# The values of two attention groups as one projection by seven products of quarters

## The chip, the cores and the metric

The kernel runs on one core of a Trainium2 chip. The metric is the device time of one execution in microseconds, as the median of several runs. Beside it stands one profiled execution, whose trace gives every instruction on the engines TensorE (PE; its weight loads are PEld), VectorE (DVE), ScalarE (ACT), GpSimd (POOL) and on the queue of SyncE (SP), which issues the transfers.

## The reference, cut to what matters

One layer of a hybrid decoder over 512 positions of width 1024, in float32. An RMSNorm gives u; one projection `u @ w_in` gives queries, keys and values of 18 attention heads, a pooling input, the inputs of a state-space mixer, and gates. The heads form three groups of six; each group attends with its own dilation:

```
ATTN_GROUPS = ((128, 1), (512, 4), (2048, 16))     # window, dilation
proj = u @ w_in[i]
q, k, v, pool_in, z, xbc, dt_raw, gate_pre = jnp.split(proj, split_idx, axis=-1)
v = v.reshape(b, s, ATTN_HEADS, HEAD_DIM)          # 18 heads of 64: 3 groups of 384 columns
```

The three branches are gated, merged and projected; a gated feed-forward layer and a final norm follow. What matters here is v: for each group, 512 x 1024 of u times 1024 x 384 of the weights. The text counts groups 1 to 3; the code counts g = 0 to 2.

## The kernel before, in words

**Products in three terms.** TensorE multiplies in a rounded float32 form, so each operand is split into a high part (the rounded value) and a low part (what rounding left), and a product is high x high, high x low and low x high: three matmuls for each block of 128 contracted rows (`mm3`, L222 to L229). u is kept turned, as `uh` and `ul`, eight blocks of 128 features by 512 positions. Weights come from memory per job: `fetch` (L170) issues the transfer into one of two `raw` buffers, `cast` (L182) makes the high part `wh` on ScalarE (L191), `lows` (L204) the low part `wl` on VectorE (L211). There are three buffers for `wh` and two for `wl`.

**Jobs and their pipeline.** The program is a list of jobs in a fixed order, and the order of instructions on TensorE, ScalarE, VectorE and GpSimd is that in which the program writes them. At the head of job n (L1459 to L1482) the loop first issues any half of a cast that is still held back (`second`), then the low part of job n+1, then sets up the cast of job n+2, then issues the transfer of job n+3, and only then writes the body of job n. The cast is cut into two column halves: `flush` (L139), called at the start of each `step`, issues one half; what is left is issued at the head of the next job.

**Steps.** `step()` (L145) lets pieces of other work in between the matmuls: after the flush it advances every generator in `running` by one stage and starts one from `waiting`. The items of attention and of the state-space mixer come in this way. An attention item (`item` in `attend`, L507) has four stages at four steps: scores on TensorE (L521, for a pair of heads at once), bias addition and row maxima on VectorE (L528 to L539), exponentials on ScalarE (L542); nothing; the transpose of the probabilities on TensorE (L548) and its copy by VectorE or ScalarE in turns (L549); for every second head the product with the values (L560). A group of attention ends with transposes of its statistics (L573).

**The order around the change** (`program`, L1277): second gates, the pooling branch and its output projection `w_b`, then per group g its values (`v_jobs`, L454), its queries and keys (`qk_jobs`, L482), and `attend(g)`, which queues the items. After group 1 the state-space preparation is put in as the sixth item that waits; after group 2 come six jobs for the convolved inputs (L673) and `ssd_start` (L842), which issues twelve Silus on ScalarE and queues the state-space items; then group 3's values, queries and keys.

`v_jobs` has two jobs per group, each with four contracted blocks and 384 columns; u is the stationary operand and the weights stream. Each job makes two steps, one after two blocks of positions. In the second job each block's result is copied out of PSUM (L466); those of groups 2 and 3 are scattered by 4 transfers each into `vr` tiles, in the order of the dilation (L477). `qk_jobs` has three jobs per group; each makes one query and one key chunk of 24 matmuls with 512 columns, and a step after each chunk.

**Products by quarters, already in use.** `down` (L1075) computes part of the feed-forward output in the way that the change extends to the values: four quarters of the activations times four quarters of the weights by seven products of sums for eight. `sums_of` (L1055) makes the sums of activations, and `diff` (L1091) those of weights, in place.

Of the kernel before, what the change touches and what calls it, by code (L numbers as in the profile page):

```python
# [10 lines left out]
F32 = mybir.dt.float32  # L11
# [5 lines left out]
P = 128  # L17
# [55 lines left out]
class Job:  # L73


    def __init__(self, parts, k, c, body):
        self.parts, self.k, self.c, self.body = parts, k, c, body
        self.raw = self.split = None
        self.late = self.short = False
        self.load = self.form = None  # L80


@with_exitstack
def trunk(ctx: ExitStack, tc, out, x, rel_bias, ln1_g, w_in, b_gate, w_a, pool_w, pool_scale, w_b,
# [23 lines left out]
    def T(name, dt=F32, shape=(P, S)):  # L108
        return big.tile(list(shape), dt, name=name, tag="t")
# [105 lines left out]
    def low(job, cuts=1, eng=None):  # L215
        for _ in lows(job, cuts, eng):
            pass

    def wsrc(w, k0, k1, c0, c1):
        return w[k0 * P:k1 * P, c0:c1].rearrange("(k p) c -> p k c", p=P)  # L220
# [10 lines left out]
    def chunk_a(ps, ws, j, xh, xl, ks, lo=0, hi=S, k0=0):  # L231
        wh, wl = ws
        mm3(ps[:, lo:hi], lambda k: wh[:, k0 + k, j * P:(j + 1) * P],
            lambda k: wl[:, k0 + k, j * P:(j + 1) * P],
            lambda k: xh(k)[:, lo:hi], lambda k: xl(k)[:, lo:hi], ks)
# [14 lines left out]
    def jobs_b(parts_of, c, xh, xl, nk, evac, kstep=4, mk=None, blocks=range(4), tail=0,  # L250
               turn_over=False, acc=None, opened=(), keep=()):

        acc = {} if acc is None else acc
        starts = list(range(0, nk, kstep))
        held = []

        def use(k0, k1, ws, tb):
            wh, wl = ws  # L260
            mm3(acc[tb][:, :c], lambda k: wh[:, k - k0, :], lambda k: wl[:, k - k0, :],
                lambda k: xh(k, tb), lambda k: xl(k, tb), range(k0, k1),
                k0 == 0 and tb not in opened, k1 == nk and tb not in keep, flip=True)

        for n, k0 in enumerate(starts):
            k1 = min(nk, k0 + kstep)

            def body(ws, n=n, k0=k0, k1=k1):
                if n == 0:
                    for tb in blocks:  # L270
                        if tb not in opened:
                            acc[tb] = (mk or MM)("pb")
                late = n >= len(starts) - tail
                if late:
                    held.append((k0, k1, ws))
                if late and n < len(starts) - 1:
                    return
                for tb in blocks:
                    for a in (held if late else [(k0, k1, ws)]):
                        use(*a, tb)  # L280
                    if k1 == nk and tb not in keep:
                        evac(tb, acc[tb])
                    if tb % 2:
                        step()
            job = Job(parts_of(k0, k1), k1 - k0, c, body)
            job.short = len(blocks) < 4
            if turn_over and n == len(starts) - 1:
                job.late = True

                def body(ws, job=job, inner=body):  # L290
                    late_split.append(job.prepare(later=True))
                    inner(ws)
                job.body = body
            yield job


    def rstd_of(ss, cols, n):
# [156 lines left out]
    def v_jobs(g):  # L454
        extra = SH if g == 0 else 0

        def parts(k0, k1):
            c = C_V + 384 * g
            r = [wsrc(w_in, k0, k1, c, c + 384)]
            if extra:  # L460
                r.append(wsrc(w_in, k0, k1, C_DT, C_DT + SH))
            return r

        def evac(tb, ps):
            t = T(f"v{g}")
            (act.copy if tb % 2 else dve.tensor_copy)(t[:, :384], ps[:, :384])  # L466
            if extra:
                dve.tensor_copy(dtr[:, tb, :], ps[:, 384:400])
            if g == 0:
                V[g, tb] = t  # L470
                return

            if tb == 0:
                for n in range(4):
                    V[g, n] = T(f"vr{g}")
            for n in range(4):
                sp.dma_start(V[g, n][32 * tb:32 * tb + 32, :384], t[n:P:4, :384])  # L477

        return jobs_b(parts, 384 + extra, lambda k, tb: uh[:, k, tb * P:(tb + 1) * P],
                      lambda k, tb: ul[:, k, tb * P:(tb + 1) * P], KD, evac)  # L480

    def qk_jobs(g):  # L482
        for i in range(3):
            def body(ws, i=i):
                for j, which in enumerate("qk"):
                    ps = MM("pqk")
                    chunk_a(ps, ws, j, uhk, ulk, range(KD))
                    t = T(f"{which}{g}")
                    if which == "q":
                        act.mul(grouped(t, g), blocked(ps, g), 0.125)  # L490
                    else:
                        dve.tensor_copy(plain(t, g), perm(ps, g))
                    QK[which, g, i] = t
                    step()
            cq, ck = C_Q + 384 * g + i * P, C_K + 384 * g + i * P
            yield Job([wsrc(w_in, 0, KD, cq, cq + P), wsrc(w_in, 0, KD, ck, ck + P)], KD, 256, body)
# [522 lines left out]
    def up_evac(m, ps):  # L1019
        t = HC[m] = T("hc")  # L1020
        act.activation(t, ps, AF.Identity, bias=ff["c1"][:, ff["b"] + m:ff["b"] + m + 1], scale=fw(2, m))  # L1021
        for k in range(2):
            sh = 2 - k
            dve.scalar_tensor_tensor(t[:, sh:], ps[:, :S - sh], fw(k, m), t[:, sh:], OP.mult, OP.add)  # L1024
        if m < KF:
            act.activation(t, t, AF.Silu)
            return
        a = HC[m - KF]
        pool.tensor_tensor(a, a, t, OP.mult)  # L1029

        def later():
            yield
            k = m - KF
            if k >= KS or k % 2:
                h, l = T("fh", F32R), T("fl", F32R)
                act.copy(h, a)
                dve.tensor_sub(l, a, h.bitcast(F32))
                ACTS[k] = (h, l)
                if k < KS:
                    yield  # L1040
                    for _ in sums_of(k // 2, HC[k - 1], a):
                        yield
                return
            if k == 0:
                wide.extend(ypool.tile([P, 4, S], F32R, name=n, tag="xs") for n in ("sh", "sl"))
            t = T("f0", F32R)
            act.copy(t[:, :256], a[:, :256])
            dve.tensor_sub(t[:, 256:], a[:, :256], t[:, :256].bitcast(F32))
            FS[0, k // 2] = (t[:, :256], t[:, 256:])

        running.append(later())

    FS = {}

    def sums_of(p, f0, f1):  # L1055


        lo, hi = slice(0, 256), slice(256, S)
        sa, sb = T("sa"), T("sb")
        dve.tensor_tensor(sa[:, lo], f0[:, hi], f1[:, hi], OP.add)  # L1060
        dve.tensor_tensor(sa[:, hi], sa[:, lo], f0[:, lo], OP.subtract)
        dve.tensor_tensor(sb[:, lo], f0[:, lo], f0[:, hi], OP.subtract)
        dve.tensor_tensor(sb[:, hi], f1[:, lo], sa[:, hi], OP.subtract)
        yield
        ah, al = (t[:, p, :] for t in wide)
        bh, bl = T("sbh", F32R), T("sbl", F32R)
        act.copy(ah, sa)
        act.copy(bh, sb)
        yield
        dve.tensor_sub(al, sa, ah.bitcast(F32))  # L1070
        dve.tensor_sub(bl, sb, bh.bitcast(F32))
        FS[1, p], FS[2, p] = (ah[:, lo], al[:, lo]), (ah[:, hi], al[:, hi])
        FS[3, p], FS[4, p] = (bh[:, lo], bl[:, lo]), (bh[:, hi], bl[:, hi])

    def down():  # L1075

# [7 lines left out]
        def load_w():  # L1084
# [2 lines left out]
                W[at] = both[:, 4 * at:4 * at + 4, :]  # L1087
                sp.dma_start(W[at], quarter(at, 1))
            get_x1()

        def diff(out, a, b):  # L1091
            dve.tensor_tensor(out, a, b, OP.subtract)
            return out

        def product(ps, ws, parts, first, last):

# [180 lines left out]
    def program():  # L1277
        yield from jobs_a(w_in, C_POOL, 8, uhk, ulk, KD, pool_evac)
        yield Call(lambda: waiting.append(rows_of_bias()))
        yield from gate_jobs(1)  # L1280
        yield from pool_out_job()
        yield from branch_jobs(1, w_b, YB, 8)
        for g in range(3):
            yield from v_jobs(g)
            yield from qk_jobs(g)
            yield Call(lambda g=g: attend(g))
            if g == 0:
                yield Call(lambda: waiting.insert(5, ssd_prep()))
            if g == 1:
                yield from jobs_a(w_in, C_XBC, 12, uhk, ulk, KD, xbc_evac)  # L1290
                yield Call(ssd_start)
# [193 lines left out]
ORDERED = {EngineType.PE, EngineType.Activation, EngineType.DVE, EngineType.Pool}  # L1485
NBIG = 54
MIX = "ZZ0zz1ggggaa"
SSD_ORDER = ((0, 0, 1), (1, 0, 1), (0, 1, 1), (2, 0, 1), (1, 1, 1), (3, 0, 1), (2, 1, 1), (3, 1, 1))
WARM = 12
# [29 lines left out]
```

## Time and profile before

| | us |
|---|---|
| median of 3 runs | 1052.53 (1052.18 to 1053.45) |
| the profiled execution | 1051.72 |
| its span, first to last instruction | 1049.5 |
| PE / DVE / ACT / POOL busy | 1038.3 / 613.5 / 442.4 / 137.8 |
| values of group 1, two jobs | 160.2 to 177.8 |
| queries and keys of group 1 | 177.8 to 210.5 |
| values of group 2, with attention items between | 210.5 to 230.4 |
| values of group 3, with items between | 354.2 to 375.4 |
| queries and keys of group 3 | 375.4 to 415.2 |

Times are in microseconds, those of single rows from the start of the span. A row of the view in order of time gives start, length, engine, line, operation, output and inputs with shapes, the number of instructions that follow each other, and in brackets how long the engine was idle before and what ended that wait. Matmuls are pipelined: the length of one is longer than the distance to the next, so the chain's pieces, not the lengths, give what a matmul costs. Operations that follow each other on VectorE also overlap a little.

### The profile page before, as it was taken

The numbers are of one execution on the slowest core, as the hardware profiler recorded it, in microseconds if no ns is written. First come the engines' busy times: TensorE is split into PE (matmuls) and PEld (weight loads), VectorE is DVE, ScalarE is ACT, GpSimd is POOL, SyncE is SP. The second block draws the span as 40 slices with busy tenths as digits, with TensorE's granted clock in tenths as the row PEclk, the third lists the DMA queues.
The fourth block names the chain that finished last, engine by engine and source line by source line (L and its number), as shares of the span: only waits on it lengthen the run. The fifth ranks groups of instructions, "written<-read, shape, count | busy, mean of one in ns | idle before, by whom it ended". The sixth has DMA issues, their size and how long they took to land.

```text
span 1049.5 us, 13068 instructions
## 1 busy us (share of the span) xinstructions
PE 1038.3 (99%) x5244; PEld 867.5 (83%) x5244; DVE 613.5 (58%) x824; ACT 442.4 (42%) x716; POOL 137.8 (13%) x118
## 2 busy tenths in 40 slices
PE   8999999999999999999999999999999999999997
PEld 8878889897888888787888888898888888878885
DVE  5552523254667548576568856766766556556545
ACT  6343411233444733466554324545444443433331
POOL 1580000000000001100134500001111111110110
PEclk9999999999999999999999999999999999999999
DMA  7236233342222355541253426643232322362332
GB/s 234 86 116 181 81 103 86 95 114 78 84 81 61 81 150 141 151 120 52 81 144 89 156 85 221 206 162 118 80 121 81 110 91 84 117 240 65 115 102 80
DMA packets 119787, 121.80 MB, mean 116 GB/s; under 512 B 5523, under 2 KB 101590, under 8 KB 119727
## 3 DMA queue, kind: packets, MB, share of 16 engines
q1 hardware_dynamic: 119727, 120.98, 37.4%
q8 instruction: 41, 0.67, 0.3%
q14 instruction: 19, 0.16, 0.0%
HBM read 115.07 MB, written 4.32 MB: 114 GB/s over the span
## 4 chain that ended last, share of the span: by engine, by line
PE 94%; issue 2%; ACT 1%; DVE 1%; DMA 1%; POOL 0%; SPq 0%; DVEq 0%; ACTq 0%; POOLq 0%
PE pa L228 35%; PE pu L228 22%; PE pb L228 17%; PE pqk L228 9%; PE p L228 2%; PE ps L521 1%; PE pu L1211 1%; PE ppw L228 1%; PE po L560 1%; PE pt L548 1%; PE py L817 1%; PE pyo L823 1%; DMA raw<-in_w_in_dram 1%; PE pst L834 0%; ACT wh L191 0%
## 5 line engine op out<-in xcount | busy, mean ns | idle before, releaser
L211 DVE TENSOR_TENSOR wl<-raw,wh 128x2048 fp32r<-128x2048 f32 (+3 forms) x95 | 217.3, 2290 | 93.1 <-ACT wh L191 54.2
L191 ACT CAST wh<-raw 128x1024 fp32r<-128x1024 f32 (+3 forms) x188 | 189.4, 1025 | 86.9 <-PE pa L228 32.9
L228 PE MATMUL pa<-uh,wh 128*128 128x512 f32 x384 | 99.3, 400 | 0.3 <-ACT wh L191 0.3
L1024 DVE SCALAR_TENSOR_TENSOR hc<-pu,fcol,hc 128x510 f32<-128x510 f32 x88 | 65.8, 748 | 51.3 <-ACT hc L1021 49.7
L228 PE MATMUL pa<-ul,wh 128*128 128x512 f32 x384 | 95.0, 389 | 0.0
L228 PE MATMUL pa<-uh,wl 128*128 128x512 f32 x384 | 94.9, 389 | 0.0
L228 PEld LDWEIGHTS pa<-ul,wh 128*128 128x128 f32 x384 | 72.1, 188 | 15.3
L228 PEld LDWEIGHTS pa<-uh,wl 128*128 128x128 f32 x384 | 72.1, 188 | 15.0
L228 PEld LDWEIGHTS pa<-uh,wh 128*128 128x128 f32 x384 | 69.9, 188 | 16.5 <-issue 1.7
L228 PE MATMUL pu<-uh,wh 128*128 128x512 f32 (+1 forms) x352 | 83.6, 379 | 0.0
L228 PE MATMUL pu<-uh,wl 128*128 128x512 f32 (+1 forms) x352 | 83.5, 379 | 0.0
L228 PE MATMUL pu<-ul,wh 128*128 128x512 f32 (+1 forms) x352 | 83.5, 379 | 0.0
L228 PEld LDWEIGHTS pu<-uh,wl 128*128 128x128 f32 x352 | 64.2, 188 | 12.5
L228 PEld LDWEIGHTS pu<-ul,wh 128*128 128x128 f32 x352 | 64.2, 188 | 12.5
L228 PEld LDWEIGHTS pu<-uh,wh 128*128 128x128 f32 x352 | 64.1, 188 | 12.4
L1021 ACT ACTIVATE hc<-pu,fcol,fcol 128x512 f32<-128x512 f32 x40 | 31.2, 780 | 75.7 <-PE pu L228 75.5
L1029 POOL TENSOR_TENSOR hc<-hc 128x512 f32<-128x512 f32 x22 | 31.5, 1432 | 223.1 <-DVE hc L1024 169.3
L796 POOL TENSOR_TENSOR xd<-xc,dec 128x512 f32<-128x512 f32 x6 | 6.4, 1064 | 361.6 <-DVE xc L787 343.0
L542 ACT ACTIVATE sb<-sb,nm 128x128 f32<-128x128 f32 (+1 forms) x72 | 30.1, 419 | 47.0 <-DVE nm L539 33.3
L919 DVE TENSOR_TENSOR sg<-sg,pa 128x512 f32<-128x512 f32 x24 | 16.1, 685 | 41.9 <-PE pa L228 41.8
L228 PE MATMUL pqk<-uh,wh 128*128 128x512 f32 x144 | 36.7, 397 | 0.0
L228 PE MATMUL pqk<-ul,wh 128*128 128x512 f32 x144 | 35.6, 389 | 0.0
(322 smaller groups left out, 1695.5 us busy)
## 6 DMA issues: line engine op xcount, KB each, us to landing
raw<-in_w_in_dram SPq DMA_DIRECT2D x25, 1024.0 KB, 5.4
raw<-in_ffn_w_up_dram SPq DMA_DIRECT2D x22, 1024.0 KB, 5.1
raw<-in_w_in_dram SPq DMA_DIRECT2D x20, 512.0 KB, 5.6
raw<-in_ffn_w_down_dram SPq DMA_DIRECT2D x10, 1024.0 KB, 5.1
raw<-in_w_o_dram SPq DMA_DIRECT2D x8, 1024.0 KB, 5.7
raw<-in_w_in_dram SPq DMA_DIRECT2D x6, 768.0 KB
raw<-in_w_b_dram SPq DMA_DIRECT2D x4, 1024.0 KB, 5.0
al<-ad SPq DMA_DIRECT2D x16, 256.0 KB, 6.3
```

Source lines behind the costliest of these rows:

```text
L191: act.copy(job.high[:, :, o], job.raw[:, :, o])
L211: (eng or dve).tensor_tensor(l[:, :, o], job.raw[:, :, o], h[:, :, o].bitcast(F32), OP.subtract)
L228: pe.matmul(ps, l, r, start=first and n == 0, stop=last and n == total - 1)
L521: pe.matmul(pss[i][:, o:o + w * P], q[r, n * P:(n + 1) * P], k[r, kb * P:(kb + w) * P], start=True, stop=True)
L542: act.activation(sb[:, off:off + w * P], sb[:, off:off + w * P], AF.Exp, bias=nm[:, n, h:h + 1], accum_out=ls[:, n, h:h + 1])
L548: pe.transpose(pt[:, o:o + P], sb[:, o:o + P], eye)
L560: pe.matmul(po[DH * hh:DH * hh + DH, n * P:(n + 1) * P], V[g, kb + i][:, (2 * c + hh) * DH:(2 * c + hh + 1) * DH], probs[2 * c + hh, nb][: ...
L817: pe.matmul(py[DH * i:DH * i + DH, j * P:(j + 1) * P], xc[:, o:o + DH], als[j // 2][:, lo:lo + P], start=True, stop=True)
L919: dve.tensor_tensor(s, s, ps, OP.mult)
L1021: act.activation(t, ps, AF.Identity, bias=ff["c1"][:, ff["b"] + m:ff["b"] + m + 1], scale=fw(2, m))
L1024: dve.scalar_tensor_tensor(t[:, sh:], ps[:, :S - sh], fw(k, m), t[:, sh:], OP.mult, OP.add)
L1029: pool.tensor_tensor(a, a, t, OP.mult)
```

## The change: what it does, and the diff

The values of groups 2 and 3 are computed together, ahead of the queries of group 2. The product is u (512 x 1024) times weights (1024 x 768), whose left 384 columns are group 2's and right ones group 3's. u is cut into first and second half of the positions, and even and odd blocks of 128 features; the weights into even and odd blocks, and left and right. Seven products of 256 positions, 512 features and 384 columns, of quarters or of their sums, give all four quarters of the result:

- `sums_of_u` makes the sums of u's quarters in 13 stages, one per step, from the head of the `w_b` jobs on: 2 + 4 + 2 VectorE operations and 2 ScalarE copies for each of four pairs of blocks. `sums_of` is now shared with the feed-forward layer, and unchanged in what it does there.
- `v_pair` loads the two right quarters into the two `xs` buffers after group 1's values; the left quarters and, for the last product, one right quarter come as ordinary jobs (five transfers of 768 KB for four).
- `sevens` makes seven jobs in the order A11, A12, 2, 3, 1, A22, 4. Each has 24 matmuls (two blocks of positions, four contracted blocks, three terms) and **one** step. Jobs 2, 3, 1 and A22 load nothing; their weights are differences formed on VectorE: three from the head of group 1's last query job on, at successive steps, and one at the cast of A22.
- Results leave PSUM by additions: 14 on VectorE and 2 copies on ScalarE, for 4 + 4 copies before. The 32 scatters stay.
- The first two query and key jobs of group 3 make a step in the middle of each chunk too (`MORE = 2`): four more steps. The old steps within group 3's values are gone.

The diff, cut to its core:

```diff
     def low(job, cuts=1, eng=None):
         for _ in lows(job, cuts, eng):
             pass
+        if job.then:
+            job.then()
...
+    LO, HI = slice(0, 256), slice(256, S)
+    def sums_of(f0, f1, ah, al, found):
+        sa, sb = T("sa"), T("sb")
+        dve.tensor_tensor(sa[:, LO], f0[:, HI], f1[:, HI], OP.add)
+        dve.tensor_tensor(sa[:, HI], sa[:, LO], f0[:, LO], OP.subtract)
+        dve.tensor_tensor(sb[:, LO], f0[:, LO], f0[:, HI], OP.subtract)
+        dve.tensor_tensor(sb[:, HI], f1[:, LO], sa[:, HI], OP.subtract)
+        yield
+        bh, bl = T("sbh", F32R), T("sbl", F32R)
+        act.copy(ah, sa)
+        act.copy(bh, sb)
+        yield
+        dve.tensor_sub(al, sa, ah.bitcast(F32))
+        dve.tensor_sub(bl, sb, bh.bitcast(F32))
...
+    def sevens(quarter, c, side, W, emit):
+        r1, r3 = {}, {}
+        def job(j, load, form, use):
+            def body(ws):
+                wh, wl = ws
+                parts = side(j)
+                for i in range(2):
+                    ps = MM("pb")
+                    o = slice(i * P, (i + 1) * P)
+                    mm3(ps[:, :c], lambda k: wh[:, k, :], lambda k: wl[:, k, :],
+                        lambda k: parts[k][0][:, o], lambda k: parts[k][1][:, o], range(4), flip=True)
+                    use(i, ps[:, :c])
+                step()
+            new = Job([load] if load is not None else [], 4, c, body)
+            new.form = form
...
+        def p1(i, ps):
+            r1[i] = T("r1")[:, :c]
+            act.copy(r1[i], ps)
+        def p6(i, ps):
+            dve.tensor_tensor(r1[i], r1[i], ps, OP.add)
+        def p7(i, ps):
+            r3[i] = T("r3")[:, :c]
+            dve.tensor_tensor(r3[i], r1[i], ps, OP.add)
+        def p5(i, ps):
+            emit(1, 1, i, r3[i], ps)
+            dve.tensor_tensor(r1[i], r1[i], ps, OP.add)
+        def forms():
+            diff(one.raw, W[0], one.raw)
+            yield
+            diff(W[0], W[1], W[0])
+            yield
+            diff(W[1], W[1], one.raw)
...
+        one = job("A11", quarter(0, 0), None, p1)
+        one.then = start
+        two = job("A12", quarter(1, 0), None, lambda i, ps: emit(0, 0, i, r1[i], ps))
+        yield one
+        yield two
+        yield job(2, None, lambda: formed(lambda: W[1]), p6)
+        yield job(3, None, lambda: W[0], p7)
+        yield job(1, None, lambda: one.raw, p5)
+        yield job("A22", None, lambda: diff(two.raw, two.raw, W[1]),
+                  lambda i, ps: emit(1, 0, i, r3[i], ps))
+        yield job(4, quarter(1, 1), None, lambda i, ps: emit(0, 1, i, r1[i], ps))
...
+    def v_pair():
+        c, W = C_V + 384, []
+        rows_ = lambda c0: w_in[:, c0:c0 + 384].rearrange("(k two p) c -> two p k c", two=2, p=P)
+        quarter = lambda two, h: rows_(c + 384 * h)[two]
...
+        def emit(hi, right, i, a, ps):
+            g, tb = 1 + right, 2 * hi + i
+            t = T(f"v{g}")
+            dve.tensor_tensor(t[:, :384], a, ps, OP.add)
+            for n in range(4):
+                if (g, n) not in V:
+                    V[g, n] = T(f"vr{g}")
+                sp.dma_start(V[g, n][32 * tb:32 * tb + 32, :384], t[n:P:4, :384])
...
     def qk_jobs(g):
...
-                    chunk_a(ps, ws, j, uhk, ulk, range(KD))
+                    if g == 2 and i < MORE:
+                        wh, wl = ws
+                        for k0 in (0, 4):
+                            mm3(ps, lambda k: wh[:, k, j * P:(j + 1) * P],
+                                lambda k: wl[:, k, j * P:(j + 1) * P], uhk, ulk, range(k0, k0 + 4),
+                                k0 == 0, k0 == 4)
+                            if k0 == 0:
+                                step()
+                    else:
+                        chunk_a(ps, ws, j, uhk, ulk, range(KD))
...
+        yield Call(lambda: running.append(sums_of_u()))
         yield from branch_jobs(1, w_b, YB, 8)
+        load, pair = v_pair()
         for g in range(3):
-            yield from v_jobs(g)
+            if g == 0:
+                yield from v_jobs(g)
+                yield Call(load)
+            if g == 1:
+                yield from pair
             yield from qk_jobs(g)
```

More of the change, by code (lines that the diff above doesn't have):

```diff
@@ L79, in __init__ @@
         self.late = self.short = False
-        self.load = self.form = None
+        self.load = self.form = self.then = None
 @with_exitstack
@@ L294, in jobs_b @@
             yield job
+    LO, HI = slice(0, 256), slice(256, S)
[12 more added lines that the diff above has]
+        dve.tensor_sub(bl, sb, bh.bitcast(F32))
+        for j, h, l, half in ((1, ah, al, LO), (2, ah, al, HI), (3, bh, bl, LO), (4, bh, bl, HI)):
+            found(j, h[:, half], l[:, half])
@@ new lines, in diff, with start, formed @@
+    def diff(out, a, b):
+        dve.tensor_tensor(out, a, b, OP.subtract)
+        return out
+    def sevens(quarter, c, side, W, emit):
[13 more added lines that the diff above has]
+            new.form = form
+            if load is None:
+                new.load = lambda: None
+            return new
+        def p1(i, ps):
[15 more added lines that the diff above has]
+            diff(W[1], W[1], one.raw)
+        def start():
+            left.append(forms())
+            next(left[0])
+            running.append(left[0])
+        def formed(w):
+            for _ in left[0]:
+                pass
+            return w()
+        left = []
+        one = job("A11", quarter(0, 0), None, p1)
[9 more added lines that the diff above has]
+        yield job(4, quarter(1, 1), None, lambda i, ps: emit(0, 1, i, r1[i], ps))
@@ new lines, in trunk, with sums_of_u, side_u @@
+    US = {}
+    def sums_of_u():
+        for p in range(4):
+            f = []
+            for k in (2 * p, 2 * p + 1):
+                f.append(T("uf"))
+                dve.tensor_tensor(f[-1], uh[:, k, :].bitcast(F32), ul[:, k, :].bitcast(F32), OP.add)
+            yield
+            yield from sums_of(*f, T("sah", F32R), T("sal", F32R),
+                               lambda j, h, l, p=p: US.__setitem__((j, p), (h, l)))
+    def side_u(j):
+        if j in QUARTER:
+            two, half = QUARTER[j]
+            return [(uh[:, 2 * p + two, half], ul[:, 2 * p + two, half]) for p in range(4)]
+        return [US[j, p] for p in range(4)]
@@ L297, in rstd_of @@
+    QUARTER = {"A11": (0, LO), "A12": (1, LO), "A22": (1, HI)}
     def rstd_of(ss, cols, n):
@@ L468, in evac, with load @@
                 dve.tensor_copy(dtr[:, tb, :], ps[:, 384:400])
[L469 to L477, printed above, removed]
+            V[g, tb] = t
         return jobs_b(parts, 384 + extra, lambda k, tb: uh[:, k, tb * P:(tb + 1) * P],
                       lambda k, tb: ul[:, k, tb * P:(tb + 1) * P], KD, evac)
+    def v_pair():
+        c, W = C_V + 384, []
+        rows_ = lambda c0: w_in[:, c0:c0 + 384].rearrange("(k two p) c -> two p k c", two=2, p=P)
+        quarter = lambda two, h: rows_(c + 384 * h)[two]
+        def load():
+            for two in range(2):
+                W.append(ypool.tile([P, 4, S], F32, name="w3", tag="xs")[:, :, :384])
+                sp.dma_start(W[two], quarter(two, 1))
+        def emit(hi, right, i, a, ps):
[6 more added lines that the diff above has]
+                sp.dma_start(V[g, n][32 * tb:32 * tb + 32, :384], t[n:P:4, :384])
+        return load, sevens(quarter, 384, side_u, W, emit)
     def qk_jobs(g):
@@ L1040, in later @@
                     yield
-                    for _ in sums_of(k // 2, HC[k - 1], a):
+                    for _ in sums_of(HC[k - 1], a, *(t[:, k // 2, :] for t in wide),
+                                     lambda j, h, l: FS.__setitem__((j, k // 2), (h, l))):
                         yield
@@ L1053, in trunk @@
     FS = {}
[L1055 to L1073, printed above, removed]
     def down():
@@ L1089, in load_w @@
             get_x1()
-        def diff(out, a, b):
-            dve.tensor_tensor(out, a, b, OP.subtract)
-            return out
         def product(ps, ws, parts, first, last):
@@ L1486 @@
 NBIG = 54
+MORE = 2
 MIX = "ZZ0zz1ggggaa"
```

## The prediction

> **What bounds the kernel now.** I read the page's first three parts, then the chain that ended last, then TensorE's own waits, then stretches around the change, then the instructions of each engine in order of time.
>
> ```profile
> PE 1038.3 (99%) x5244; PEld 867.5 (83%) x5244; DVE 613.5 (58%) x824; ACT 442.4 (42%) x716; POOL 137.8 (13%) x118
> PEclk9999999999999999999999999999999999999999
> PE 94%; issue 2%; ACT 1%; DVE 1%; DMA 1%; POOL 0%; SPq 0%; DVEq 0%; ACTq 0%; POOLq 0%
> ```
>
> TensorE is busy 99% of the span at full granted clock, and 94% of the chain is its work. So a matmul less is worth its own pitch, and any new wait of TensorE costs its full length. The next view gives stretches of the old kernel: length, then busy time of PE, PEld, DVE, ACT, POOL, granted clock, DMA share, GB/s.
>
> ```profile
> 116.00:178.00 62.00, 62.00 (x294) 54.36 (x293) 20.83 (x21) 12.42 (x16) 0.00 (x0) 1.00 0.35 95
> 210.50:230.00 19.50, 19.50 (x119) 18.47 (x119) 11.22 (x18) 6.03 (x17) 0.00 (x0) 1.00 0.50 129
> 354.00:376.00 22.00, 21.57 (x143) 20.50 (x142) 10.15 (x11) 15.38 (x25) 1.04 (x1) 1.00 0.42 110
> ```
>
> The values of group 2 lie in 210.5 to 230, those of group 3 in 354 to 376, beside twelve Silus on ScalarE; the only TensorE idle time there is 0.43 us. The new sums of the input fall into 116 to 178, where VectorE is busy a third of the time.
>
> **What is saved.** The pieces of the chain give the pitch of the value matmuls:
>
> ```profile
> 210.47 4.19 PE pb L228 x24
> 214.66 1.06 PE ps L521 x8
> 215.72 8.54 PE pb L228 x48
> ```
>
> 24 matmuls of 384 columns take 4.19 us, 174.6 ns each; the 334 ns of one matmul's row overlap the next. After a break the first ones add 0.16 us (8.54 against 2 x 4.19). Before, there are 4 jobs x 4 blocks x 4 k x 3 terms = 192 such matmuls; after, 7 x 2 x 4 x 3 = 168. **Saved: 24 x 174.6 ns = 4.19 us.** The 144 matmuls of the third queries and keys stay as many, and the attention items (their score, transpose and output matmuls) stay the same and only move.
>
> **What is added off the path.** The sums of u: per pair of row blocks 2 + 2 VectorE operations of 128x512 (nearest row: the 0.69 us score addition of that shape) and 4 of 128x256 (the 0.42 us one), 4.4 us, in all 17.8 us on VectorE, and 8 ScalarE copies of 0.58 us. They go over 13 steps from 116 to 183. VectorE has 62.0 - 20.8 = 41 us free there, and a step adds 2.8 us at most to about 1.8 us of work in 5.4 us: cost 0. Without that cover a low part would come late by under 1 us. Transfers: five of 768 KB for four, and the same 32 scatters of values on SP's queue: 0, because the 16 engines are half busy in this stretch. The first two formed weights are made during the last first-group query job, where VectorE idles 8.5 us: 0.
>
> **What is added on the path: a ring of VectorE and ScalarE.** A new job lasts only 24 matmuls, 4.19 us, and makes one step. So the program order at each step is: ScalarE casts the first column half of the weights two jobs ahead, then come the attention item's exponentials, then the second half (it is flushed at the head of the next job). VectorE can make the low part only then, and in its queue the job's two results and the next item's addition and row maxima stand behind that low part; the next exponentials wait for these maxima. So the low part of one job waits, round both engines, for that of the job before. These rows of the old kernel price the ring (start, length):
>
> ```profile
> 215.76 0.69 DVE L535 TENSOR_TENSOR sb<-ps,b 128x512 f32<-128x512 f32 x1 [2.89 <-PE ps L521]
> 216.48 0.69 DVE L539 TENSOR_REDUCE nm<-sb 128x2 f32<-128x512 f32 x1
> ...
> 217.21 0.51 ACT L542 ACTIVATE sb<-sb,nm 128x256 f32<-128x256 f32 x1 [6.16 <-DVE nm L539]
> ...
> 218.21 1.04 ACT L191 CAST wh<-raw 128x1024 fp32r<-128x1024 f32 x1
> ...
> 230.34 1.05 ACT L191 CAST wh<-raw 128x1024 fp32r<-128x1024 f32 x1
> ...
> 231.43 2.29 DVE L211 TENSOR_TENSOR wl<-raw,wh 128x2048 fp32r<-128x2048 f32 x1 [1.95 <-ACT wh L191]
> ```
>
> Addition to maxima 0.72, maxima 0.69, hand-over 0.04, exponentials 1.00, and a cast follows at once; the last pair shows VectorE idle for exactly such a cast. In the new shapes: half a cast 0.82 (row 128x768), low part 1.75 (row 128x1536, next operation 0.08 earlier), one addition of a 128x384 result from PSUM: a copy of that shape takes 0.55, the next starting 0.47 after it, and rows of 256 and 512 columns take 0.42 and 0.69, so 0.47 of pitch, bounds 0.35 to 0.69. A subtraction of two quarters, 128x1536: no row; the low part has its shape, so 1.75, bounds 0.55 and 2.29. One turn is 1.67 + 2 x 0.47 + 0.72 + 0.69 + 0.04 + 1.00 + 0.82 + 0.04 = 5.9 us, 0.5 to 0.6 more when VectorE also copies a transpose, 1.7 more when it forms the sixth weights, 0.9 more behind the fifth product's four additions. TensorE's turn is 4.19 + 0.16 and that step's items (scores 1.06 or 0.85, transposes 0.33 to 0.44, output 1.02), 5.4 us on average.
>
> Played out on the old clock, from 210.47. A job needs the high part of its weights at its start and the low part 8 x 174.6 ns = 1.4 us (and 0.16) later. Columns: high part ready, low part ready, TensorE starts, it ends with the step's items, its waits.
>
> | job | high | low | start | end with items | wait |
> |---|---|---|---|---|---|
> | 1 | ready | ready | 210.5 | 215.7 | 0 |
> | 2 | ready | 214.6 | 215.7 | 220.1 | 0 |
> | 3 | 219.0 | 220.8 | 220.1 | 225.6 | 0 |
> | 4 | 225.0 | 226.7 | 225.6 | 230.3 | 0 |
> | 5 | 231.0 | 232.8 | 231.0 | 238.3 | 0.7 + 0.2 + 0.3 |
> | 6 | 238.0 | 239.8 | 238.3 | 243.0 | 0 |
> | 7 | 245.4 | 247.2 | 245.4 | 251.2 | 2.4 + 0.2 |
>
> The 0.3 is an output matmul behind a ScalarE copy that stands behind the sixth cast. The seventh weights' transfer can start when the fifth low part frees its buffer, 232.8, and lands at 238.2 (5.4 us, the 1024 KB row), 5 us before the exponentials ahead of the second half-cast: not late. The results wait in PSUM for VectorE up to 6 us; four buffers hold two jobs, and each is read before the job after next starts. Counting the 54 big tiles, the fifth job wants one or two more than there are, for the third group's scattered values; their transfers alone wait, until that job's sums are free, and nobody needs them before the third attention. **Waits of TensorE in the seven jobs: 3.8 us**, of which 2.4 stand ahead of the seventh. Bounds: 0 if the two engines ran so far ahead that the ring never closed; about 8 if every operation had its full length with no overlap, each hand-over 0.1 us, and the subtraction 2.29. I take 3.8, because most terms are rows of their own shape. After it, the second queries' steps are 6.7 us apart and the ring opens again.
>
> A page speaks to the wait of 2.4 us. All PEclk rows here are at full rate, with no gap longer than 1.1 us. The Trainium skill, "TensorE: Matmul & The Clock Gate", section "Why this matters for your kernels", advises against idle gaps of more than about 3 us between bursts, since the clock then halves; by it a gap of 2.4 us would just escape and the sum would stay, while one half as long again would add the last rival below; no row of before shows such a gap.
>
> **The third queries.** Group 3's values no longer lie behind the Silus. The first step now comes 2.74 us (12 x 228.6 ns) after the convolved inputs' last matmul, and its transposes need the first Silu. ScalarE's rows put addition 0.78, cast 1.04 and table load 1.28 ahead of it, and it takes 0.6: 3.7 us, against 2.9 with the break's 0.16, so a wait of 0.85. The old wait of 0.43 behind an attention output's copy goes, as that item ends three steps earlier (7 + 6 + 12 steps for 4 + 6 + 12). Net **+0.4**; bounds -0.4 and +4. What is late next there: the state-space rows' transfer (6.3 us to landing) and VectorE behind it; by the same playing-out the first product over them comes four steps, some 13 us, after the issue and waits for nothing.
>
> **Sum.** -4.19 + 3.8 + 0.4 = 0.0 us. The profiled execution took 1051.72 (span 1049.5 and 2.2 around it) and would stay there; the median of the runs is 1052.53, 0.8 above it, and I put the forecast on that: **1052.5**.
>
> **Rivals.** A measurement of this kernel can tell about 0.2%, 2.1 us, from no change, so 1050.4 and 1054.6 divide the cases.
> - *Forecast: the ring gives back about what the products save* (waits 1.7 to 5.9 us): 1050.4 to 1054.6. Chance 0.45.
> - *The ring stays covered*, faster. For it: VectorE is 58% busy, ScalarE 42%, and ScalarE casts far ahead wherever nothing binds it. Against: order ties the second half-cast behind the exponentials. Waits 0 to 1.7: 1052.5 - 4.2 + 0.4 = 1048.7, up to 1050.4. Chance 0.22.
> - *The ring is longer than played*, slower: each 0.1 us more per turn costs 0.4 us over four turns, so it decides from 0.5 us per turn on (waits over 5.9): 1054.6 to 1057. For it: hand-overs are counted at 0.04. Chance 0.17.
> - *The denser steps of the third queries stall the state-space items*: VectorE has waited up to 6.6 us for their rows. If half of that reaches TensorE: +3 to +4, 1055.5 to 1056.5. Chance 0.1.
> - *A wait long enough halves the clock*: if the seventh job then ran at half rate, 24 x 174.6 ns more, 1056.7 and above. Chance 0.06.
>
> Faster 0.22, within 0.45, slower 0.17 + 0.10 + 0.06 = 0.33. The range 1049.0 to 1057.5 leaves out the end of a fully covered ring and the sum of several slow cases.
>
> **What would show it.** Right: 168 matmuls of 384 columns for the two groups; TensorE waits for the high part of the weights in the fifth and seventh new jobs, about 4 us in all, with VectorE's low parts 6 to 7.7 us apart; VectorE idle before them until the cast; one wait of under 1 us for a Silu. Wrong: no TensorE wait in the seven jobs (faster), waits spread over all of them or over the third queries (slower), or a granted clock below full after 245.

## The result, and the profile after

The changed kernel took 1056.07 us (median of 8 runs, 1055.27 to 1058.59) against 1052.74 of the kernel before: ratio 1.0034, interval 1.0023 to 1.0045. It is slower by 0.34%. The forecast was 1052.5. The time lies inside the range, yet the sum had come to no change, and the loss is clear.

The profiled execution took 1055.72, its span is 1053.8 (1049.5 before). The page's first part and the chain that ended last:

```profile
PE 1038.7 (99%) x5220; PEld 865.3 (82%) x5220; DVE 645.9 (61%) x873; ACT 450.9 (43%) x728; POOL 137.6 (13%) x118
PE 84%; DVE 5%; ACT 3%; DMA 3%; issue 3%; SPq 1%; POOL 1%; DVEq 0%; ACTq 0%; POOLq 0%
```

TensorE has 24 matmuls fewer, yet its busy time has not fallen. TensorE's share of the chain went from 94% to 84%: VectorE, ScalarE and transfers now set its times in places. TensorE's own waits (total, times, longest) and three stretches (length, then busy time of PE, PEld, DVE, ACT, POOL, granted clock, DMA share, GB/s) say where:

```profile
PE pb L230 <- ACT wh L191: 2.6, 2, 2.1
PE pbt L904 <- ACT xcv L986: 1.0, 1, 1.0
PE pb L230 <- DVE wl L211: 0.5, 1, 0.5
PE po L702 <- ACT sb L691: 0.3, 1, 0.3
```

```profile
240.00:255.00 15.00, 12.89 (x70) 11.66 (x69) 9.44 (x13) 5.71 (x10) 0.00 (x0) 0.89 0.74 191
255.00:292.00 37.00, 36.64 (x198) 28.88 (x197) 23.14 (x55) 16.95 (x42) 0.00 (x0) 1.00 0.44 128
366.00:412.00 46.00, 44.97 (x235) 36.08 (x234) 28.45 (x54) 25.01 (x36) 4.24 (x4) 1.00 0.46 128
```

In the old kernel the stretch from 230 to 272 had no idle TensorE time, and its clock was 1.00:

```profile
230.00:272.00 42.00, 42.00 (x237) 33.67 (x237) 21.28 (x50) 16.46 (x39) 0.00 (x0) 1.00 0.28 86
```

In the changed kernel 240 to 255 has both, 2.1 us of idle TensorE and a clock of 0.89. The instructions in order of time show how they belong together (start, length, engine, operation, idle before and its releaser):

```profile
242.23 0.49 PE L690 MATMUL pt<-eye,sb 128*128 128x128 f32 x3
244.83 1.10 PE L230 MATMUL pb<-wh,sbh 128*128 128x384 f32 x4 [2.11 <-ACT wh L191]
245.73 1.48 PE L230 MATMUL pb<-wh,sbl 128*128 128x384 f32 x4
247.01 1.48 PE L230 MATMUL pb<-wl,sbh 128*128 128x384 f32 x4
248.29 1.15 PE L230 MATMUL pb<-wh,sbh 128*128 128x384 f32 x4
249.28 0.87 PE L230 MATMUL pb<-wh,sbl 128*128 128x384 f32 x4
```

After the gap four matmuls take 1.48 us for 0.85, and in stretches of 1 us the granted clock is half:

```profile
245.00:246.00 1.00, 1.00 (x5) 1.00 (x6) 1.00 (x1) 1.00 (x2) 0.00 (x0) 0.75 0.38 108
246.00:247.00 1.00, 1.00 (x4) 1.00 (x4) 1.00 (x3) 0.10 (x1) 0.00 (x0) 0.50 0.28 84
247.00:248.00 1.00, 1.00 (x5) 1.00 (x5) 0.50 (x2) 0.78 (x1) 0.00 (x0) 0.50 0.10 34
248.00:249.00 1.00, 1.00 (x5) 1.00 (x4) 0.70 (x1) 0.27 (x1) 0.00 (x0) 0.54 0.16 50
249.00:250.00 1.00, 1.00 (x8) 1.00 (x7) 1.00 (x1) 0.00 (x0) 0.00 (x0) 1.00 0.73 152
```

A busy TensorE at half clock counts as busy, which is part of why its busy time did not fall. From the starts of TensorE's groups in both traces, from the first value job (210.31 before, 209.93 after) to the last chunk of the third keys' end (415.01 and 417.86), the account is:

| term | us |
|---|---|
| value matmuls without waits, 34.14 to 29.82 | -4.32 |
| waits in the seven jobs: 0.78, 0.49, 0.11, 2.35 | +3.73 |
| seventh job at half clock, 5.96 for 4.28 | +1.68 |
| output and scores at 270 to 275: 1.72 for 1.02, 1.82 for 1.06 | +1.46 |
| wait for the first Silu 1.05, old wait of 0.56 gone | +0.49 |
| third queries cut by four more steps, 33.19 to 33.71 | +0.52 |
| convolved inputs' chunks, cut less often, 67.38 to 67.18 | -0.20 |
| sum (the stretches differ by 3.23) | +3.36 |

The profiled executions differ by 4.3 us in all: the changed one is 0.4 us earlier at the first value job and loses another 1.5 us behind the third keys. The medians differ by 3.3 us.

The 1.46 us were foreseen by nothing in the prediction. VectorE's and SP's rows there:

```profile
249.03 5.44 SPq L610 DMA_DIRECT2D vr<-v  x8
254.58 0.43 SPq L842 DMA_DIRECT2D dr<-in_ssd_d_dram  x1
```

```profile
256.09 0.21 DVE L845 COPY dr<-dr 8x128 f32<-8x128 f32 x1 [3.10 <-DMA dr<-in_ssd_d_dram]
```

The load of a small row for the state-space preparation stands on SP's queue behind eight scatters of the sixth job's results. These results leave PSUM late, from 246.5 on, and the scatters, from the first to the last, take 5.44 us to issue. VectorE waits 3.1 us for the row, with an attention item and the next low part behind it. Two steps later TensorE finds a probability copy and, as far as the order of VectorE's copies shows, a PSUM tile not ready.

### The profile page after: what moved, and what is told of

It reads as the page before. It is cut to its first block, busy times and chain, and to the rows that moved or that the text cites. A ratio compares the mean times of both kernels' runs of the same rounds, so it can differ in the third digit from the quotient of the medians.

```text
span 1053.8 us, 13084 instructions
## 1 busy us (share of the span) xinstructions
PE 1038.7 (99%) x5220; PEld 865.3 (82%) x5220; DVE 645.9 (61%) x873; ACT 450.9 (43%) x728; POOL 137.6 (13%) x118
## 3 DMA queue, kind: packets, MB, share of 16 engines
HBM read 115.86 MB, written 4.32 MB: 114 GB/s over the span
## 4 chain that ended last, share of the span: by engine, by line
PE 84%; DVE 5%; ACT 3%; DMA 3%; issue 3%; SPq 1%; POOL 1%; DVEq 0%; ACTq 0%; POOLq 0%
PE pa L230 31%; PE pu L230 22%; PE pb L230 15%; PE pqk L230 8%; PE p L230 2%; DMA raw<-in_w_in_dram 2%; DVE wl L211 2%; ACT wh L191 1%; PE ppw L230 1%; PE po L702 1%; PE ps L663 1%; PE pt L690 1%; PE py L959 1%; PE pyo L965 1%; DMA raw<-in_ffn_w_up_dram 1%
## 5 line engine op out<-in xcount | busy, mean ns | idle before, releaser
L230 PE MATMUL pqk<-uh,wl 128*128 128x512 f32 x144 | 36.2, 389 | 0.0
```

The source lines that it names most:

```text
L230: pe.matmul(ps, l, r, start=first and n == 0, stop=last and n == total - 1)
```

## The experiments

Theory *order*: the second half-cast behind the exponentials closes the ring, and the rest follows from its lag. Rival *load*: VectorE simply has more to do in seven short jobs than they can cover. Each kernel starts from the changed one unless told otherwise. Ratios are to the kernel before in the same comparison (there 1052.16 in the first four, 1051.98 in the others); the change's own is 1.0034.

**1. Both half-casts ahead of the items.**

```diff
                     use(i, ps[:, :c])
+                flush()
                 step()
```

> The changed kernel, but each of the seven jobs issues both halves of the held-back cast before its step's items, not one before and one after them. Same work on every engine. Theory 'order': the waits of the seven jobs (3.7 us with their hand-overs) and the half clock that follows the longest (1.7 us) go, so 1056.1 - 5.4 = 1050.7, up to 1051.5 if part of a wait stays; full granted clock from 230 to 254. Rival 'load': VectorE simply has too much to do in the seven jobs, whatever stands ahead of the second half-cast; then nothing changes, 1055.5 to 1056.5, and the waits stay.

Measured: 1049.08, ratio 0.9967 (0.9954 to 0.9979), faster than the kernel before. In the changed kernel the second half of the seventh cast (the first of the two at 243.97) stands behind the exponentials, which wait for VectorE, and the low part waits for that half:

```profile
242.97 0.51 ACT L684 ACTIVATE sb<-sb,nm 128x256 f32<-128x256 f32 x1 [4.79 <-DVE nm L681]
243.97 1.76 ACT L191 CAST wh<-raw 128x768 fp32r<-128x768 f32 x2
```

```profile
244.81 1.76 DVE L211 TENSOR_TENSOR wl<-raw,wh 128x1536 fp32r<-128x1536 f32 x1 [1.94 <-ACT wh L191]
```

The same place in this run, ScalarE's rows, VectorE's rows and two stretches:

```profile
232.36 1.55 ACT L191 CAST wh<-raw 128x768 fp32r<-128x768 f32 x2
237.99 0.51 ACT L685 ACTIVATE sb<-sb,nm 128x256 f32<-128x256 f32 x1 [4.08 <-DVE nm L682]
```

```profile
237.20 0.69 DVE L682 TENSOR_REDUCE nm<-sb 128x2 f32<-128x512 f32 x1
237.81 1.75 DVE L211 TENSOR_TENSOR wl<-raw,wh 128x1536 fp32r<-128x1536 f32 x1
```

```profile
240.00:255.00 15.00, 15.00 (x88) 12.76 (x87) 10.14 (x19) 7.02 (x14) 0.00 (x0) 1.00 0.75 190
255.00:292.00 37.00, 37.00 (x203) 29.89 (x202) 21.52 (x49) 14.73 (x38) 0.00 (x0) 1.00 0.30 90
```

Both halves of the cast are done before the exponentials, the low part follows the row maxima without a wait, and TensorE is busy throughout at full clock. The same work for VectorE in another order: *load* falls. More was won than I expected, because the wait at 270 to 275 went too (the small row still loads behind the scatters, but 7 us earlier). The trace wins 6.7 us up to the third keys, the 3.73 + 1.68 + 1.46 of the table less 0.2.

**2. The gap filled with idle work**, ahead of the seventh job:

```diff
                     ps = MM("pb")
+                    if j == 4 and i == 0:
+                        for _ in range(9):
+                            pe.matmul(ps[:, :P], ones, ones, start=True, stop=True)
```

> The changed kernel with nine matmuls of 128x128 (of ones, 0.23 us each, overwritten by the product that follows) ahead of the seventh job, in the 2.1 us in which TensorE waits. They add work only where it idles. Theory 'idle gap halves the clock': granted clock stays full from 245 to 249 and the seventh job takes 4.3 us for 6.0, so 1056.1 - 1.7 = 1054.4. Rival 'the clock fell for another reason than the gap': it falls again, 1056.1, or 1056.3 with a little overrun.

Measured: 1056.29, ratio 1.0041 (1.0027 to 1.0055): no gain. The profiled execution, which took 1054.53, shows the full clock all the same, and where its gain went (stretch 240 to 255, and a wait of TensorE):

```profile
240.00:255.00 15.00, 14.78 (x94) 13.09 (x93) 9.39 (x13) 5.83 (x10) 0.00 (x0) 1.00 0.74 191
```

```profile
PE po L705 <- ACT sb L694: 1.2, 1, 1.2
```

The second queries start 1.1 us earlier, but the output matmul at 270 takes 2.62 us from start to next for 1.72: the wait there is pinned to the transfers and to VectorE, so time saved ahead of it is given back: 0.2 us are left by the next chunk. The expected 1054.4 missed that. This explains the trace, not the median: the other four executions, of which there is no trace, took 1055.70 to 1058.07 at mean granted clocks of 0.995 to 0.997, against 0.998 here. Their clock fell more than this one's; where is not known.

**3. The four extra steps one chunk later.**

```diff
-                    if g == 2 and i < MORE:
+                    if g == 2 and (i, j) in MORE:
...
-MORE = 2
+MORE = ((0, 1), (1, 0), (1, 1), (2, 0))
```

> The changed kernel with its four extra steps in the third queries one chunk later (none in the first query chunk, one in the third job's query chunk). Theory 'Silu': the first state-space step comes 5.5 us after the convolved inputs and no longer waits 1.05 us for the first Silu: 1056.1 - 1.05 = 1055.0. Rival 'the wait only moves', to the items four steps on, which have one chunk less or more of cover: 1056.0 to 1056.5.

Measured: 1054.14, ratio 1.0015 (1.0006 to 1.0024). The wait for the Silu is gone: the chunk takes 5.44 us and its transposes follow at once.

```profile
379.80 1.98 PE L230 MATMUL pqk<-uh,wl 128*128 128x512 f32 x8
381.62 0.60 PE L904 MATMUL pbt<-eye,xcv 128*128 128x128 f32 x4
```

Up to the third keys' end the trace wins only 0.7 us, as the wait at 270 was 0.5 longer in this execution; no new wait appears in the third queries. The rival falls. The ratio fell by 0.0019, or 2.0 us, more than the trace shows; each ratio's interval is about 1 us to either side, so the size of the gain rests on the trace.

**4. The two small rows loaded early**, into one big tile.

```diff
+    def prep_rows():
+        t = T("dr")
+        dr, gr = t[:, :P + 2], t[:, 2 * P:3 * P]
+        sp.dma_start(dr[:8, P:], ssd_d[0].rearrange("(c h) -> c h", h=2))
+        sp.dma_start(gr[:8, :P], ssd_norm_w[0].rearrange("(c p) -> c p", p=P))
+        cst["rows"] = dr, gr
...
                 yield Call(load)
+                yield Call(prep_rows)
```

> The changed kernel with the two small rows that the state-space preparation needs loaded after the first group's values (into one big tile for two), not behind the scatter of the sixth job's results on SP's queue. Theory 'queue': VectorE's wait of 3.1 us for them and TensorE's 1.46 us at 270 to 275 (a probability copy and a PSUM tile) go: 1056.1 - 1.5 = 1054.6. Rival 'VectorE is behind anyway after the seven jobs': it waits for the next low part instead and TensorE still loses over 1 us there: 1055.5 to 1056.2.

Measured: 1053.36, ratio 1.0010 (1.0001 to 1.0019). The clock still halves, the wait behind it is gone:

```profile
240.00:255.00 15.00, 12.91 (x71) 11.72 (x69) 11.49 (x19) 6.09 (x12) 0.00 (x0) 0.89 0.75 191
255.00:292.00 37.00, 37.00 (x204) 29.64 (x203) 21.56 (x51) 16.83 (x40) 0.00 (x0) 1.00 0.45 128
```

The trace wins 1.47 us up to the third keys' end, the table's term. So the cause there is the place on SP's queue together with the lag; either taken away is enough.

**5. All three repairs.**

> The changed kernel with all three repairs: both half-casts ahead of the items, the small rows loaded early, the four extra steps one chunk later. Theory: the first repair alone took the waits of the seven jobs, the half clock and the wait at 270 to 275 (1049.1); of the others only the Silu's wait is left to take, 0.7 to 1.05 us: 1048.0 to 1048.4, with no TensorE wait over 0.3 us between 205 and 412. Rival: the steps' shift only moves a wait, as it moved none of the rest: 1049.1 or above.

Measured: 1047.79, ratio 0.9958 (0.9945 to 0.9970), the best version. TensorE is busy in all of 366 to 412 (46.00 of 46.00), and its trace lists no wait of TensorE between 205 and 412. Against the first repair alone the intervals overlap; by the traces the rest wins 1.3 us up to the third keys' end, of which the Silu's wait is 1.05.

**6. The gap filled and the rows early.**

> The changed kernel with the gap ahead of the seventh job filled by nine small matmuls and the small rows loaded early. The gap's filling alone kept the clock full but its 1.2 us were given back to the next wait at 270. Theory: with that wait gone they are kept: 1.2 us under the rows alone (1053.4), 1052.2. Rival: another wait pins TensorE to VectorE's and ScalarE's times further on, and it stays at 1053.4.

Measured: 1052.63, ratio 1.0006 (0.9997 to 1.0014), against 1.0010 with the rows alone: in the expected direction, within the intervals. The trace decides: from the transposes ahead of the seventh job to that job's end 7.41 us for 8.53, and from the first value job to the third keys' end 205.31 for 206.46. So 1.1 us are kept once nothing behind them waits. The mean granted clock over the eleven executions is 0.9984, for 0.9974 with the rows alone.

**7. The gap half filled.**

> The same with four small matmuls for nine: TensorE idles about 1.2 us ahead of the seventh job in place of 2.1. A look at the granted clock from 244 to 250: full if the clock falls only after an idle stretch longer than that, half for 3.3 us if 1.2 us are enough already.

Measured: one execution, 1052.91. TensorE idles 1.2 us, the granted clock is 1.00 from 244 to 250, and the matmuls behind the gap take their usual time:

```profile
244.70 0.97 PE L230 MATMUL pb<-wh,sbh 128*128 128x384 f32 x4 [1.20 <-ACT wh L191]
245.50 0.86 PE L230 MATMUL pb<-wh,sbl 128*128 128x384 f32 x4
```

**8. The old kernel with the sums of u**, unused.

> The kernel before, with the sums of u's quarters made at the same steps as in the change, and used by nothing: 17.8 us more of VectorE and 4.7 of ScalarE from 116 to 183. Theory: they lie beside TensorE's work and cost nothing, ratio 1.000. Rival: VectorE's added work delays low parts and costs 1 us or more, ratio 1.001 or above.

Measured: 1051.52, ratio 0.9997 (0.9988 to 1.0006). VectorE's busy time from 116 to 178 rises from 20.8 to 35.0 us, and TensorE stays busy:

```profile
116.00:178.00 62.00, 62.00 (x294) 54.35 (x293) 35.00 (x51) 16.23 (x22) 0.00 (x0) 1.00 0.35 95
```

## Why the prediction was wrong, point by point

- *Saved matmuls, 4.19 us:* right; 4.32 in the trace.
- *Sums and formed weights at nothing:* right for the sums (experiment 8); the first formed weights lie ahead of the ring, as played out, and TensorE does not wait before the fifth job.
- *The ring, 3.8 us, with 2.4 ahead of the seventh job:* right in mechanism, place and size: 3.73, with a gap of 2.11 and the low part's hand-over. Experiment 1 shows the cause, the order of the half-casts. The ring alone would have given nearly the forecast.
- *"by it a gap of 2.4 us would just escape":* this step failed. The clock halved after 2.11 us of idle TensorE, which followed three transposes. The rival had a chance of 0.06 and a price of 4.2 us, a whole job at half rate; it came, at 1.68 us, as the clock was back after 3.4 us. In the Trainium skill, "TensorE: Matmul & The Clock Gate", section "Why this matters for your kernels", the bound is about 3 us; here 2.11 was enough, and the measurement decides. A granted clock below full after 245 was among the prediction's own signs of being wrong.
- *"After it, the second queries' steps are 6.7 us apart and the ring opens again":* this step failed too, by 1.46 us, a wait that the sum had at nothing. I looked at the casts and low parts behind the seven jobs, not at what SP's queue had behind the late scatters. The prediction asked whether the scatters' tiles or the next weights would be late, but not whether a small load of other work stood behind them. Experiments 1 and 4 show it.
- *The third queries, +0.4:* right, 0.49. Missing were the breaks that the four extra steps add, 0.5 us, less 0.2 elsewhere.
- *The rival of a longer ring, and that of a stalled state-space mixer:* neither came; the ring's turns went as played, and no state-space product waited.

Two more things belong to the clock. The old trace held a warning that the prediction's "no row of before shows such a gap" passed over: at the program's end TensorE's last matmul ends at 1042.6, and 2.1 us later the granted clock falls to half.

```profile
1044.00:1045.00 1.00, 0.00 (x0) 0.00 (x0) 0.57 (x4) 0.36 (x3) 0.00 (x0) 0.87 0.01 2
1045.00:1046.00 1.00, 0.00 (x0) 0.00 (x0) 0.93 (x4) 0.00 (x0) 0.00 (x0) 0.50 0.00 0
```

And the 1.68 us are those of the profiled execution. The mean granted clocks of the eight executions range from 0.995 to 0.999. A mean that rounds to 0.999 leaves room for 3.2 us at half clock in all, less than one such fall of 3.4, so at least one execution did not pay it.

So the terms that were priced held within 0.2 us, and the miss is, in the profiled execution, the sum of three that were put at nothing: clock 1.68, queue 1.46 and breaks 0.3. The loss of 1.5 us behind the third keys stays open. The largest part lies from 559 to 577, where the low part for `w_a` comes late behind VectorE operations of 128x4 that took 0.94 and 1.22 us (1.27 and 0.16 in the kernel before). This stretch lasted 17.15 us in the changed kernel, 17.27 in the fourth, 17.35 in the fifth and 17.08 in the seventh experiment, against 16.47 to 16.51 in the kernel before and the others. Its cause was not tried; the other 0.8 us lie in two smaller differences, ahead of 643 and of 932.

## What to carry to other kernels

When a job gets shorter, play its turn out on every in-order engine, with what the program writes between the two halves of a preparation: here one line of order, not the amount of work, decided between +0.34% and -0.33%. Price a wait of TensorE with what comes after it too: the half clock and the loads that stand on a shared queue behind late results cost here almost as much as the waits themselves. A gap's cost that is pinned further on to another engine is not won by mending it alone.

## What the runs showed of the hardware that I had not expected

The changed kernel and experiments 3 and 4 left TensorE idle for 2.1 us ahead of the seventh job. In all three traces its granted clock fell to one half up to 0.7 us after the idle stretch had ended, 2.1 to 2.8 us after it had begun, and was back after 3.4 to 3.5 us. With the stretch filled (experiments 2 and 6), or with 1.2 us of it left (experiment 7, one execution), the clock did not fall there.

At the end of the program, where TensorE has nothing left to do, the clock falls in all ten profiled executions, but at different times: 2.1 to 5.2 us after the last matmul. So the length of an idle stretch alone does not say when the clock falls. Where the bound lies, and whether the three transposes ahead of the gap (0.49 us) counted as idle, was not tried.
